# The value projection of the stick-breaking branch in 512 columns, two row tiles at a time

## The chip, the core and the metric

The kernel runs on one core of one Trainium2 chip. The metric is the device time of one execution in microseconds (us): the median of three runs, and beside it one execution that was taken with the hardware profiler, from which every row below comes. TensorE is called PE here, VectorE DVE, ScalarE ACT, GpSimd POOL, and SP is the engine that issues most transfers.

## What is computed

One layer of a decoder trunk on 512 tokens of width 1024. Cut to what matters for the change:

```python
h    = rms_norm(x, g_mix)                       # 512 x 1024
proj = h @ w_in                                 # 1024 x 5120
qa, ka, va, qb, kb, vb, gates = split(proj)     # each of the first six is 512 wide
ya = moba_attention(qa, ka, va)                 # 8 heads of 64
yb = stick_breaking_attention(qb, kb, vb)       # 8 heads of 64
m  = sigmoid(gate_a) * (ya @ W_a) + sigmoid(gate_b) * (yb @ W_b)
x  = x + m @ W_out                              # then a ConvGLU and a last RMSNorm
```

Here `vb`, the values of the second branch, is a product of 512 rows (four row tiles of 128) with 1024 x 512 weights. The change touches how this one product is cut up.

## The kernel before

Every large product is done three times, in pieces that keep float32 accuracy: each operand is split into a high and a low part, and `mm3` (lines 72 to 75) issues high x high, high x low, low x high into one PSUM tile. Weights come in blocks of 128 x 1024 float32 by one transfer each. `wload` (line 56) issues the transfer into a tile of the pool `wraw` (five deep), lets ACT write the high part (`whi`, line 68) and DVE the low part (`wlo`, line 69) into tiles of the pool `wsp` (three deep for each name, so a new block's split has to wait until PE is through with the block three loads earlier).

The middle of the kernel (63 to 240 us) weaves two kinds of work on PE. The attention proper is `attend`: for a pair of head pairs it goes through a list of nine pieces (scores of a group of query tiles, then turning the weights, at line 407) and ends with the product with the values (`av`, line 429). Between the pieces PE is given projections, as generators in the list `fillers`; `fill(n)` takes n steps from them. A step of 1.0 is three matmuls of 512 columns (the 256-column form of `vproj_b` yields 0.5 for three matmuls). The numbers n stand in GAPS_A, GAPS_A2 and GAPS_B. Order of the fillers: the second half of the first branch's q and k, q and k of pairs 0 and 1, `vproj_b(0)`, q and k of pairs 2 and 3, `vproj_b(1)`, and the first gate projections. PE's order is exactly the order in which the code is written (`manual_schedule`, line 50). The other engines' instructions are put in order by a scheduler that models their times when the program is built.

The projections write to PSUM tiles named `mm`, from `pmm`, two banks deep, used in turn. A third tile can be begun only when the first has been copied out. `vproj_b(g)` does half of the columns (256) for one row tile after the other: two row tiles share one bank, 48 matmuls, and are then copied out to `vb`, one half by ACT (line 251), one by DVE (line 252). So the bank of one pair of tiles is emptied while PE fills the other.

In the second branch DVE runs, for each group of scores, scans (line 378) and products (line 380) over the attention weights, after ACT's sigmoids (lines 364 and 366) and POOL's masks (line 370). DVE and ACT also empty the `av` tile into `ya` or `yb` (lines 435 and 436) and q and k of the second branch are copied out by DVE as `o` (lines 304 and 306).

Of the kernel before, what the change touches and what calls it, by code (L numbers as in the profile page):

```python
# [10 lines left out]
F32 = mybir.dt.float32  # L11
F32R = mybir.dt.float32r
BF = mybir.dt.bfloat16
AF = mybir.ActivationFunctionType
OP = mybir.AluOpType
# [3 lines left out]
S = 512  # L19
D = 1024  # L20
KT = D // 128
QT = S // 128
# [4 lines left out]
NWARM = 9 * (448,) + (128,)  # L27
NP = FT // 2
NL = 3
WORDER = ([(n, k) for n in ("qk0", "va") for k in range(4)] + [("vb", g, h) for g in range(2) for h in range(2)]  # L30
          + [("mqk", n, i) for n in range(2) for i in range(2)] + [("sqk", p, n) for p in range(4) for n in range(2)]
          + [("g", i, b) for i in range(KT) for b in range(2)] + [("ab", i) for i in range(KT)]
          + [("out", k) for k in range(KT)] + [("ox", j) for j in range(KT // 2)] + [("up", i, b) for i in range(FT) for b in range(2)]
# [6 lines left out]
def trunk_layer(ctx: ExitStack, tc: tile.TileContext, x: bass.AP, xT: bass.AP, w: bass.AP, vec: bass.AP,  # L40
                gfin: bass.AP, trig: bass.AP, out: bass.AP):
    nc = tc.nc

    def pool(stack, name, bufs, space=None, side=None):
        kw = {}
        if space is not None:
            kw["space"] = space
        if side is not None:
            kw["side"] = side
        return stack.enter_context(tc.tile_pool(name=name, bufs=bufs, reuse_waits="tile", **kw))  # L50
# [2 lines left out]
    consts = pool(ctx, "consts", 1)  # L53
    wraw = pool(ctx, "wraw", 5)
    wsp = pool(ctx, "wsp", 3)
    def wload(key, pieces=1, eng=None):
        raw = wraw.tile([128, 1024], F32, name="raw")
        hi = wsp.tile([128, 1024], F32R, name="whi")
        lo = wsp.tile([128, 1024], F32R, name="wlo")
        n = 1024 // pieces  # L60
        for i in range(pieces):
            sl = slice(i * n, (i + 1) * n)
            (eng if eng is not None and i == 0 else nc.sync).dma_start(raw[:, sl], w[WIDX[key]][:, sl])
            if eng is not None and i == 0:
                nc.scalar.preload_act_table_set("sqrt_and_others")
        for i in range(pieces):
            sl = slice(i * n, (i + 1) * n)
            nc.scalar.activation(hi[:, sl], raw[:, sl], AF.Copy)  # L68
            nc.vector.tensor_sub(lo[:, sl], raw[:, sl], hi[:, sl].bitcast(F32))  # L69
        return hi, lo  # L70

    def mm3(ps, a, b, start, stop, **kw):
        nc.tensor.matmul(ps, a[0], b[0], start=start, stop=False, **kw)  # L73
        nc.tensor.matmul(ps, a[0], b[1], start=False, stop=False, **kw)  # L74
        nc.tensor.matmul(ps, a[1], b[0], start=False, stop=stop, **kw)  # L75

    def blk(t, k, n=128):
        return t[0][:, k * n:(k + 1) * n], t[1][:, k * n:(k + 1) * n]
# [23 lines left out]
    xg = [hp.tile([128, 2, S], F32R, name=f"xg{k}") for k in range(KT)]  # L102
    rb = hp.tile([128, S], F32, name="rb")
    asta = ExitStack()
    vp = pool(asta, "vp", 1)
    vb = vp.tile([128, QT, 512], F32, name="vb")
# [27 lines left out]
    pmm = pool(psA, "pmm", 2, PSUM)  # L134
# [7 lines left out]
    qk0 = [p1.tile([128, S], F32, name=f"q{j}") for j in range(4)]  # L142
# [18 lines left out]
    for k in range(KT):  # L161
# [7 lines left out]
        else:  # L169
            if k % 2 == 0:  # L170
# [3 lines left out]
                                             op0=OP.mult, op1=OP.subtract)  # L174
# [60 lines left out]
        use(ps)  # L235
        yield 1.0

    def vproj_b(g):
        wt = tuple(wload(("vb", g, h)) for h in range(2))
        for t in range(QT):  # L240
            if t % 2 == 0:
                ps = pmm.tile([128, S], F32, name="mm")
            o = ps[:, (t % 2) * 256:(t % 2 + 1) * 256]
            for k in range(KT):
                a = (xg[k][:, 0, t * 128:(t + 1) * 128], xg[k][:, 1, t * 128:(t + 1) * 128])
                mm3(o, a, blk(wt[k // 4], k % 4, 256), k == 0, k == KT - 1)
                if k < KT - 1:
                    yield 0.5
            if t % 2:
                dst = vb[:, t - 1:t + 1, g * 256:(g + 1) * 256]  # L250
                nc.scalar.activation(dst[:, 0], ps[:, :256], AF.Copy, scale=r1[:, t - 1:t])
                nc.vector.tensor_scalar(dst[:, 1], o, r1[:, t:t + 1], None, op0=OP.mult)
            yield 0.5

    def fill(n):
        while n > 0 and fillers:
# [35 lines left out]
    def moba_qk(g):  # L292
        for n in range(2):
            half = {}
            for i in range(2):
                yield from proj(("mqk", n, i), lambda ps: rotate(g, n, i, ps, half))
# [146 lines left out]
    st1.close()  # L443
    atp = pool(asta, "atp", 2)
    att = pool(asta, "att", 2)
    psc = pool(psA, "psc", 2, PSUM)
    ptr = pool(psA, "ptr", 1, PSUM)
    def gates(i):
# [9 lines left out]
            yield from proj(("g", i, b), lambda ps: use(b, ps))  # L458

    pend = {}  # L460
    fillers = [moba_qk(1), sb_qk(0), sb_qk(1), vproj_b(0), sb_qk(2), sb_qk(3), vproj_b(1)]
    fillers += [gates(i) for i in range(NG)]
    GAPS_A = (12, 0, 5, 5, 0, 5, 7, 5, 5)
    GAPS_A2 = (10, 0, 3, 6, 0, 3, 6, 3, 3)
    GAPS_B = (8, 4, 5, 4, 3, 5, 7, 5, 5)
    attend("a", (0, 1), GAPS_A)
    attend("a", (2, 3), GAPS_A2, True)
# [2 lines left out]
    for p in range(4):  # L470
        yhl["b", p] = ybp.tile([128, 2, S], F32R, name=f"yb{p}")
    gsig = pool(ysta, "gsig", 6, side="right")
    attend("b", (0, 1), GAPS_B)
    attend("b", (2, 3), GAPS_B)
    fill(1000)
    psA.close()
# [3 lines left out]
    pmm = pool(psB, "pmm2", 6, PSUM)  # L480
# [390 lines left out]
def pack(w_in, w_a, w_b, w_out, w_up, w_down):  # L871
    def rows(m, c):
        return m[:, c].reshape(m.shape[0] // 128, 128, len(c)).transpose(1, 0, 2).reshape(128, -1)

    c128 = np.arange(128)
    t = {}

    def halves(base, g, i):
        return base + (4 * g + c128 // 32) * 64 + 32 * i + c128 % 32

    first = np.concatenate([halves(base, 0, i) for base in (0, 512) for i in range(2)])
    for k in range(4):
        t["qk0", k] = rows(w_in[k * 256:(k + 1) * 256], first)
    for n, base in enumerate((0, 512)):
        for i in range(2):
            t["mqk", n, i] = rows(w_in, halves(base, 1, i))
    for j in range(4):
        t["va", j] = rows(w_in[j * 256:(j + 1) * 256], 1024 + np.arange(512))
    for g in range(2):
        for h in range(2):  # L890
            t["vb", g, h] = rows(w_in[h * 512:(h + 1) * 512], 2560 + g * 256 + np.arange(256))
    for p in range(4):
        for n, base in enumerate((1536, 2048)):
            t["sqk", p, n] = rows(w_in, base + p * 128 + c128)
    for i in range(KT):
        for b in range(2):
            t["g", i, b] = rows(w_in, 3072 + b * 1024 + i * 128 + c128)
        t["ab", i] = np.concatenate([rows(w_a, i * 128 + c128), rows(w_b, i * 128 + c128)], axis=1)
        t["out", i] = w_out[i * 128:(i + 1) * 128]
    for j in range(KT // 2):  # L900
        t["ox", j] = np.concatenate([w_out[(2 * j + b) * 128:(2 * j + b + 1) * 128, 512:] for b in range(2)], axis=1)
    for i in range(FT):
        for b in range(2):
            t["up", i, b] = rows(w_up, b * FF + i * 128 + c128)
        t["down", i] = w_down[i * 128:(i + 1) * 128]
    for j in range(NP):
        t["dx", j] = np.concatenate([w_down[(2 * j + b) * 128:(2 * j + b + 1) * 128, 512:] for b in range(2)], axis=1)
    return np.ascontiguousarray(np.stack([t[k] for k in WORDER]))

# [27 lines left out]
```

## Time and profile before

| what | value |
|---|---|
| median of three runs | 724.46 us (724.16 to 724.82) |
| the profiled execution | 725.84 us |
| its span on the core | 724.1 us |
| PE busy in the span | 714.9 us, 99% |
| DVE busy in the span | 554.3 us, 77% |
| ACT busy in the span | 346.5 us, 48% |
| PE's share of the chain that ended last | 94% |

The profiled execution lies 1.4 us above the median, and 1.7 us of it lie outside the span. A matmul's listed time (some 390 ns at 512 columns) overlaps its neighbour's. What PE really takes for one is the distance from its start to the next one's start, so starts are compared in all that follows, and a PE that is busy at every moment is a PE that has no listed wait.

### The profile page before, as it was taken

What the parts mean: (1) busy time and instruction counts of PE and PEld (TensorE: products, weight loads), DVE (VectorE), ACT (ScalarE), POOL (GpSimd) and SP (SyncE); (2) the same over time, 40 slices, a digit from 0 to 9 for tenths busy, and PEclk for the clock granted to TensorE, in tenths of its full rate; (3) what the DMA queues carried; (4) which work ended last, traced back from release to release, by engine and by line L of the source; (5) the groups of instructions that cost most, each with busy time, mean ns of one, the idle gap of its engine ahead of it and who ended that gap; (6) DMA issues with size and microseconds to landing.
All of it is one profiled execution on the core that took longest, in us unless ns stands there. A gap on an engine that the chain in (4) does not pass through costs nothing.

```text
span 724.1 us, 9746 instructions
## 1 busy us (share of the span) xinstructions
PE 714.9 (99%) x3792; PEld 593.3 (82%) x3792; DVE 554.3 (77%) x796; ACT 346.5 (48%) x507; POOL 22.7 (3%) x40
## 2 busy tenths in 40 slices
PE   9999999999999999999999999999999999999996
PEld 6888888879888888888888888888888888788784
DVE  7678867594873654669878787787787789888997
ACT  6335435463663232337384444443444444556664
POOL 0000000230310000000000000000000000000000
PEclk9999999999999999999999999999999999999998
DMA  8522111021122323235744223223223323467703
GB/s 305 195 88 80 67 49 69 31 88 59 60 91 68 104 87 98 82 112 180 281 153 140 90 88 109 95 88 108 96 88 102 101 88 103 138 220 226 273 29 118
DMA packets 25679, 84.11 MB, mean 116 GB/s; under 512 B 2848, under 2 KB 3616, under 8 KB 25632
## 3 DMA queue, kind: packets, MB, share of 16 engines
q1 hardware_dynamic: 25344, 83.15, 34.0%
q8 instruction: 30, 0.49, 0.3%
q10 hardware_dynamic: 288, 0.33, 0.1%
q14 instruction: 17, 0.14, 0.1%
HBM read 79.27 MB, written 4.19 MB: 115 GB/s over the span
## 4 chain that ended last, share of the span: by engine, by line
PE 94%; DVE 3%; ACT 1%; DMA 1%; issue 0%; ACTq 0%
PE b L74 13%; PE b L75 12%; PE b L73 12%; PE mm L73 11%; PE mm L74 11%; PE mm L75 11%; PE c L74 4%; PE c L73 4%; PE c L75 4%; PE q L188 3%; PE tp L429 2%; PE tp L407 2%; PE sc L330 1%; PE sc L340 1%; DMA raw<-w 1%; PE v L74 1%
## 5 line engine op out<-in xcount | busy, mean ns | idle before, releaser
L68 ACT ACTIVATE whi<-raw 128x1024 fp32r<-128x1024 f32 (+2 forms) x98 | 98.2, 1008 | 167.5 <-PE b L74 80.7
L74 PE MATMUL b<-h,whi 128*128 128x512 f32 x352 | 137.1, 389 | 0.3 <-DVE h L634 0.3
L73 PE MATMUL b<-h,whi 128*128 128x512 f32 x352 | 137.1, 390 | 0.0
L75 PE MATMUL b<-h,wlo 128*128 128x512 f32 x352 | 136.9, 389 | 0.0
L69 DVE TENSOR_TENSOR wlo<-raw,whi 128x1024 fp32r<-128x1024 f32 (+2 forms) x98 | 112.9, 1157 | 14.6 <-ACT whi L68 14.4
L73 PE MATMUL mm<-xg,whi 128*128 128x512 f32 x224 | 89.9, 401 | 0.0
L75 PE MATMUL mm<-xg,wlo 128*128 128x512 f32 x224 | 87.4, 390 | 0.0
L74 PE MATMUL mm<-xg,whi 128*128 128x512 f32 x224 | 87.3, 390 | 0.0
L74 PEld LDWEIGHTS b<-h,whi 128*128 128x128 f32 x352 | 66.1, 188 | 14.2 <-DVE h L634 0.7
L75 PEld LDWEIGHTS b<-h,wlo 128*128 128x128 f32 x352 | 66.1, 188 | 13.8
L73 PEld LDWEIGHTS b<-h,whi 128*128 128x128 f32 x352 | 66.1, 188 | 13.6
L556 ACT ACTIVATE whi<-raw 128x1024 fp32r<-128x1024 f32 x45 | 46.6, 1051 | 34.0 <-DVE raw L568 21.1
L556 DVE TENSOR_TENSOR wlo<-raw,whi 128x1024 fp32r<-128x1024 f32 x45 | 54.3, 1218 | 4.4 <-ACT whi L556 4.4
L725 DVE TENSOR_TENSOR u<-b,rb 128x512 f32<-128x512 f32 x44 | 30.3, 691 | 30.4 <-PE b L75 30.3
L73 PEld LDWEIGHTS mm<-xg,whi 128*128 128x128 f32 x224 | 42.1, 188 | 10.2 <-issue 1.8
L75 PEld LDWEIGHTS mm<-xg,wlo 128*128 128x128 f32 x224 | 42.0, 188 | 9.1
L74 PEld LDWEIGHTS mm<-xg,whi 128*128 128x128 f32 x224 | 42.2, 188 | 7.8
L727 ACT ACTIVATE t<-u,vecs 128x512 f32<-128x512 f32 x44 | 35.2, 802 | 2.1 <-DVE u L725 2.1
L74 PE MATMUL c<-wlo,xa 128*128 128x512 f32 x88 | 34.3, 390 | 0.4 <-DVE wlo L556 0.4
L73 PE MATMUL c<-whi,xa 128*128 128x512 f32 x88 | 34.2, 389 | 0.0
L75 PE MATMUL c<-whi,xa 128*128 128x512 f32 x88 | 34.2, 389 | 0.0
L730 DVE SCALAR_TENSOR_TENSOR t<-u,vecs,t 128x510 f32<-128x510 f32 x44 | 32.9, 749 | 1.3
(222 smaller groups left out, 1261.6 us busy)
## 6 DMA issues: line engine op xcount, KB each, us to landing
raw<-w SPq DMA_DIRECT2D x133, 512.0 KB, 3.3
xk<-xT SPq DMA_DIRECT2D x8, 256.5 KB, 5.3
x<-x SPq DMA_DIRECT2D x4, 512.0 KB, 7.1
x1D<-x SPq DMA_DIRECT2D x8, 256.0 KB, 3.4
x1R<-x1D SPq DMA_DIRECT2D x4, 512.0 KB, 8.0
raw<-w SPq DMA_DIRECT2D x6, 256.0 KB, 5.8
out<-on SPq DMA_DIRECT2D x6, 256.0 KB, 2.3
tg<-trig SPq DMA_DIRECT2D x1, 512.0 KB, 6.8
```

What stands on the lines that cost most here:

```text
L68: nc.scalar.activation(hi[:, sl], raw[:, sl], AF.Copy)
L69: nc.vector.tensor_sub(lo[:, sl], raw[:, sl], hi[:, sl].bitcast(F32))
L73: nc.tensor.matmul(ps, a[0], b[0], start=start, stop=False, **kw)
L74: nc.tensor.matmul(ps, a[0], b[1], start=False, stop=False, **kw)
L75: nc.tensor.matmul(ps, a[1], b[0], start=False, stop=stop, **kw)
L188: nc.tensor.matmul(qk0[c], w0[i][:, (k % 2) * 512 + c * 128:(k % 2) * 512 + (c + 1) * 128], xg[k][:, j], start=(k == 0 and n == 0), stop=( ...
L407: nc.tensor.transpose(tp[:, h, c:c + 128], a[:, h, c:c + 128], ident)
L429: nc.tensor.matmul(av[h * 64:(h + 1) * 64, j, qt * 128:(qt + 1) * 128], v[:, kb, (2 * p + h) * 64:(2 * p + h + 1) * 64], aT[p][:, h, o + k ...
L556: splits.append((nc.scalar.activation(hi, raw, AF.Copy), nc.vector.tensor_sub(lo, raw, hi.bitcast(F32))))
L725: nc.vector.tensor_mul(u, ps, rb2)
L727: nc.scalar.activation(t, u, AF.Identity, bias=cb[:, c:c + 1], scale=cw[:, 2, c:c + 1])
L730: nc.vector.scalar_tensor_tensor(t[:, 2:], u[:, :S - 2], cw[:, 0, c:c + 1], t[:, 2:], op0=OP.mult, op1=OP.add)
```

## The change

`vproj_b` takes no half any more. It does all 512 columns, for two row tiles (`T` = 0: tiles 0 and 1, then `T` = 1: tiles 2 and 3) that each fill one of the two banks of `pmm` at the same time. It goes through the four weight blocks (256 rows of the weights each, 512 columns), and with each block does the first tile, then the second. The blocks are loaded in the first round and kept for the second: three in `wsp`, the fourth in a pool of its own, `vbw`. There are 96 matmuls of 512 columns where there were 192 of 256. A round ends with a copy of the first tile by ACT and of the second by DVE, each 128 x 512, and the next round begins in the same two banks. The weights are packed in another shape to match; the number and size of the transfers stay. All of `vproj_b` stands ahead of q and k of pairs 2 and 3 in `fillers`, and the first pass of the second branch has its own, larger gaps (52 steps in place of 46), so that those projections are done by its end.

```diff
-WORDER = ([(n, k) for n in ("qk0", "va") for k in range(4)] + [("vb", g, h) for g in range(2) for h in range(2)]
+WORDER = ([(n, k) for n in ("qk0", "va", "vb") for k in range(4)]
...
-    def wload(key, pieces=1, eng=None):
+    def wload(key, pieces=1, eng=None, p=wsp):
         raw = wraw.tile([128, 1024], F32, name="raw")
-        hi = wsp.tile([128, 1024], F32R, name="whi")
-        lo = wsp.tile([128, 1024], F32R, name="wlo")
+        hi = p.tile([128, 1024], F32R, name="whi")
+        lo = p.tile([128, 1024], F32R, name="wlo")
...
-    def vproj_b(g):
-        wt = tuple(wload(("vb", g, h)) for h in range(2))
-        for t in range(QT):
-            if t % 2 == 0:
-                ps = pmm.tile([128, S], F32, name="mm")
-            o = ps[:, (t % 2) * 256:(t % 2 + 1) * 256]
-            for k in range(KT):
-                a = (xg[k][:, 0, t * 128:(t + 1) * 128], xg[k][:, 1, t * 128:(t + 1) * 128])
-                mm3(o, a, blk(wt[k // 4], k % 4, 256), k == 0, k == KT - 1)
-                if k < KT - 1:
-                    yield 0.5
-            if t % 2:
-                dst = vb[:, t - 1:t + 1, g * 256:(g + 1) * 256]
-                nc.scalar.activation(dst[:, 0], ps[:, :256], AF.Copy, scale=r1[:, t - 1:t])
-                nc.vector.tensor_scalar(dst[:, 1], o, r1[:, t:t + 1], None, op0=OP.mult)
-            yield 0.5
+    def vproj_b():
+        wts = []
+        for T in range(2):
+            ps = [pmm.tile([128, S], F32, name="mm") for _ in range(2)]
+            for j in range(4):
+                if T == 0:
+                    wts.append(wload(("vb", j), p=vbw if j == 3 else wsp))
+                for i in range(2):
+                    t = 2 * T + i
+                    for k in range(2 * j, 2 * j + 2):
+                        a = (xg[k][:, 0, t * 128:(t + 1) * 128], xg[k][:, 1, t * 128:(t + 1) * 128])
+                        mm3(ps[i], a, blk(wts[j], k % 2, 512), k == 0, k == KT - 1)
+                        if k < KT - 1:
+                            yield 1.0
+                    if j == 3:
+                        if i:
+                            nc.vector.tensor_scalar(vb[:, t], ps[i], r1[:, t:t + 1], None, op0=OP.mult)
+                        else:
+                            nc.scalar.activation(vb[:, t], ps[i], AF.Copy, scale=r1[:, t:t + 1])
+                        yield 1.0
...
+    vbw = pool(asta, "vbw", 1)
+    vbw.tile([128, 12], F32, name="gap")
...
-    fillers = [moba_qk(1), sb_qk(0), sb_qk(1), vproj_b(0), sb_qk(2), sb_qk(3), vproj_b(1)]
+    fillers = [moba_qk(1), sb_qk(0), sb_qk(1), vproj_b(), sb_qk(2), sb_qk(3)]
...
+    GAPS_B1 = (8, 4, 6, 5, 3, 6, 8, 6, 6)
     GAPS_B = (8, 4, 5, 4, 3, 5, 7, 5, 5)
...
-    attend("b", (0, 1), GAPS_B)
+    attend("b", (0, 1), GAPS_B1)
```

Three pieces of the instruction order, before and after; numbers behind a name tell tiles apart.

Place 1, PE, where the projection of pair 1's k ends and `vproj_b` begins, in the first branch's last pass. Before (`mm_1229` is that k, `mm_1333` the first pair of row tiles, `tp_1346` a turning of weights), around the first turning behind it:

```order
L75 MATMUL mm_1333<-whi_1322,xg3_95 128x256
L407 MATMUL tp_1346<-ident_67,a1_1197 128x128 x6
L73 MATMUL mm_1333<-whi_1328,xg4_96 128x256
L74 MATMUL mm_1333<-wlo_1329,xg4_96 128x256
L75 MATMUL mm_1333<-whi_1328,xg4_96 128x256
L73 MATMUL mm_1333<-whi_1328,xg5_97 128x256
```

After (`mm_1233` is that k, `mm_1325` and `mm_1326` are row tiles 0 and 1, which share the block `whi_1328`):

```order
L75 MATMUL mm_1233<-xg7_99,wlo_1229 128x512
L73 MATMUL mm_1325<-whi_1328,xg0_92 128x512
L74 MATMUL mm_1325<-wlo_1329,xg0_92 128x512
L75 MATMUL mm_1325<-whi_1328,xg0_92 128x512
L73 MATMUL mm_1325<-whi_1328,xg1_93 128x512
L74 MATMUL mm_1325<-wlo_1329,xg1_93 128x512
L75 MATMUL mm_1325<-whi_1328,xg1_93 128x512
L411 MATMUL tp_1339<-ident_67,a1_1201 128x128 x6
L73 MATMUL mm_1326<-whi_1328,xg0_92 128x512
L74 MATMUL mm_1326<-wlo_1329,xg0_92 128x512
L75 MATMUL mm_1326<-whi_1328,xg0_92 128x512
```

Before, the work behind the turning goes on in the tile begun ahead of it. After, it begins a second tile, `mm_1326`, which takes the bank that `mm_1233` had.

Place 2, PE, at the start of the second branch's first pass, behind its first scores. Before (`mm_1404` is the second pair of row tiles, `mm_1598` the next projection, q of pair 2):

```order
L73 MATMUL mm_1404<-whi_1328,xg7_99 128x256
L74 MATMUL mm_1404<-wlo_1329,xg7_99 128x256
L75 MATMUL mm_1404<-whi_1328,xg7_99 128x256
L73 MATMUL mm_1598<-xg0_92,whi_1593 128x512
L74 MATMUL mm_1598<-xg0_92,whi_1593 128x512
L75 MATMUL mm_1598<-xg0_92,wlo_1594 128x512
```

After (`mm_1326` is row tile 1, `mm_1558` and `mm_1559` are row tiles 2 and 3):

```order
L73 MATMUL mm_1326<-whi_1412,xg7_99 128x512
L74 MATMUL mm_1326<-wlo_1413,xg7_99 128x512
L75 MATMUL mm_1326<-whi_1412,xg7_99 128x512
L73 MATMUL mm_1558<-whi_1328,xg0_92 128x512
L74 MATMUL mm_1558<-wlo_1329,xg0_92 128x512
L75 MATMUL mm_1558<-whi_1328,xg0_92 128x512
L73 MATMUL mm_1558<-whi_1328,xg1_93 128x512
L74 MATMUL mm_1558<-wlo_1329,xg1_93 128x512
L75 MATMUL mm_1558<-whi_1328,xg1_93 128x512
L73 MATMUL mm_1559<-whi_1328,xg0_92 128x512
```

Before, a new tile begins in the bank that had been left 48 matmuls earlier. After, `mm_1559` begins six matmuls behind the end of `mm_1326`, whose bank it takes.

Place 3, DVE, in the same stretch. Before (`R` are the scans, `a2` the products with them, `ya2` and `ya3` the results of the first branch):

```order
L436 TENSOR_TENSOR ya2_87<-tp_1451,ya2_87 128x512
L378 SCALAR_TENSOR_TENSOR R_1548<-a1_1536 128x128
L436 TENSOR_TENSOR ya3_88<-tp_1451,ya3_88 128x512
L378 SCALAR_TENSOR_TENSOR R_1548<-a1_1536 128x128
L378 SCALAR_TENSOR_TENSOR R_1548<-a1_1536 128x256 x2
L380 TENSOR_TENSOR a2_1538<-a2_1538,R_1548 128x2x128
L380 TENSOR_TENSOR a2_1538<-a2_1538,R_1548 128x2x256
L378 SCALAR_TENSOR_TENSOR R_1569<-a1_1557 128x128 x2
L378 SCALAR_TENSOR_TENSOR R_1569<-a1_1557 128x256 x2
L252 TENSOR_SCALAR vb_104<-mm_1404,n1r_339 128x256
```

After:

```order
L440 TENSOR_TENSOR ya2_87<-tp_1424,ya2_87 128x512
L382 SCALAR_TENSOR_TENSOR R_1521<-a1_1509 128x128
L440 TENSOR_TENSOR ya3_88<-tp_1424,ya3_88 128x512
L382 SCALAR_TENSOR_TENSOR R_1521<-a1_1509 128x128
L382 SCALAR_TENSOR_TENSOR R_1521<-a1_1509 128x256 x2
L384 TENSOR_TENSOR a2_1511<-a2_1511,R_1521 128x2x128
L254 TENSOR_SCALAR vb_104<-mm_1326,n1r_339 128x512
L384 TENSOR_TENSOR a2_1511<-a2_1511,R_1521 128x2x256
```

The copy of a `vb` tile stands behind the first product with the scans after the change, and stood four scans and one product later before it. Both copies stand behind all the scans of the first pair.

## Rows read from the trace of the kernel before

**Rows 1.** Window: length, PE busy (instructions), granted clock, transfer share, GB/s.

```profile
60.00:240.00 180.00, 180.00 (x1381) 1.00 0.20 65
```

**Rows 2.** PE by time, a stretch of 256 columns: start, length, instruction, count.

```profile
119.51 0.82 PE L407 MATMUL tp<-ident,a 128*128 128x128 f32 x6
120.08 0.36 PE L73 MATMUL mm<-whi,xg 128*128 128x256 f32 x1
...
124.47 1.03 PE L407 MATMUL tp<-ident,a 128*128 128x128 f32 x8
125.26 0.36 PE L73 MATMUL mm<-whi,xg 128*128 128x256 f32 x1
```

**Rows 3.** PE by time, a stretch of 512 columns.

```profile
110.51 0.48 PE L73 MATMUL mm<-xg,whi 128*128 128x512 f32 x1
...
114.73 0.82 PE L407 MATMUL tp<-ident,a 128*128 128x128 f32 x6
```

**Rows 4.** PE by time, undisturbed stretches of either width.

```profile
104.09 0.39 PE L73 MATMUL mm<-xg,whi 128*128 128x512 f32 x1
...
104.77 0.39 PE L73 MATMUL mm<-xg,whi 128*128 128x512 f32 x1
...
121.47 0.28 PE L75 MATMUL mm<-whi,xg 128*128 128x256 f32 x1
...
121.83 0.28 PE L75 MATMUL mm<-whi,xg 128*128 128x256 f32 x1
```

**Rows 5.** DVE by time, behind the last scores of the first branch.

```profile
117.40 2.36 DVE L348 TENSOR_REDUCE st<-sc 128x2 f32<-128x1024 f32 x2 [2.80 <-PE sc L330]
119.67 0.68 DVE L306 TENSOR_TENSOR o<-mm,rb 128x512 f32<-128x512 f32 x1
...
121.26 1.22 DVE L69 TENSOR_TENSOR wlo<-raw,whi 128x1024 fp32r<-128x1024 f32 x1
```

**Rows 6.** PE by time, where vproj_b begins, and around av and the first scores.

```profile
118.09 0.28 PE L73 MATMUL mm<-whi,xg 128*128 128x256 f32 x1
...
130.60 4.59 PE L429 MATMUL tp<-aT,va 128*64 128x128 f32 x80
...
136.69 0.39 PE L73 MATMUL mm<-whi,xg 128*128 128x256 f32 x1
```

**Rows 7.** DVE by time, the first scores of the second branch.

```profile
138.46 0.60 DVE L378 TENSOR_TENSOR_SCAN R<-a 128x128 f32<-128x128 f32 x1 [1.91 <-POOL a L370]
138.99 0.66 DVE L436 TENSOR_TENSOR ya<-tp,ya 128x512 fp32r<-128x512 f32 x1
139.57 1.90 DVE L378 TENSOR_TENSOR_SCAN R<-a 128x128 f32<-128x128 f32 x3
141.39 1.36 DVE L380 TENSOR_TENSOR a<-a,R 128x256 f32<-128x256 f32 x2
```

**Rows 8.** Groups of DVE instructions, 30 to 245 us: shapes, count, busy us, mean ns, idle.

```profile
L380 DVE TENSOR_TENSOR a<-a,R 128x256 f32<-128x256 f32 x4 | 2.1, 536 | 0.0
L215 DVE TENSOR_SCALAR va<-mm,n1r 128x512 f32<-128x512 f32 x1 | 0.8, 751 | 0.6 <-PE mm L75 0.6
```

**Rows 9.** A wait of PE on DVE elsewhere, DVE and PE by time.

```profile
32.17 0.69 DVE L131 COPY rb<-mm 128x512 f32<-128x512 f32 x1 [1.66 <-PE mm L130]
...
32.92 0.50 PE L73 MATMUL mm<-whi,xg 128*128 128x512 f32 x1
```

**Rows 10.** Windows at the end (columns PE, PEld, DVE, ACT, POOL, clock), and PE at the start.

```profile
716.00:720.00 4.00, 1.31 (x6) 0.75 (x4) 3.28 (x12) 2.46 (x6) 0.00 (x0) 1.00 0.76 292
720.00:724.10 4.10, 0.00 (x0) 0.00 (x0) 0.29 (x1) 0.35 (x1) 0.00 (x0) 0.56 0.34 133
...
1.30 3.65 PE L145 MATMUL mm<-warmb 128*128 128x448 bf16 x10 [1.30 <-DVE R L375]
5.12 2.99 PE L188 MATMUL q<-xg,whi 128*128 128x512 f32 x8 [0.17 <-ACT whi L68]
...
8.86 1.98 PE L188 MATMUL q<-xg,whi 128*128 128x512 f32 x8
```

More of the change, by code (lines that the diff above doesn't have):

```diff
@@ L887, in pack @@
     for j in range(4):
[L888 to L891, printed above, removed]
+        for n, base in (("va", 1024), ("vb", 2560)):
+            t[n, j] = rows(w_in[j * 256:(j + 1) * 256], base + np.arange(512))
     for p in range(4):
```

## The prediction

> **What bounds the kernel now.** I read the page's shares first, then PE's waits, then PE and DVE by time around the places that the change touches. PE is busy for all of the 180 us from 60 to 240 us, at the full granted clock [rows 1]: in the whole stretch in which `vproj_b` runs, nothing that DVE, ACT, POOL or a transfer does holds PE up. So time is won there only by making PE's own work shorter, and every wait of PE that the change brings is lost in full, because behind it there is no idle time that could shrink.
>
> **What the change takes off PE.** 192 matmuls of 256 columns become 96 of 512. The columns streamed are the same, so the gain can only be what a matmul costs beside its columns. Undisturbed, three of 256 go from 121.47 to 121.83, 0.120 us each, and three of 512 from 104.09 to 104.77, 0.227 us each [rows 4]. Then 192 x 0.120 = 23.0 us become 96 x 0.227 = 21.8 us, 1.3 us less. With the turnings in between, 36 of 256 take from 120.08 to 124.47, 4.39 us [rows 2], and 18 of 512, the same work, from 110.51 to 114.73, 4.22 us [rows 3]; this is 0.17 us per 36, times 192/36 is 0.9 us. The first ignores the slower starts behind a turning and the second takes one stretch with much traffic for all. I take 1.0 us and keep 0.9 to 1.3.
>
> The Trainium skill, "TensorE: Matmul & The Clock Gate", section "Back-to-back issue gap", has a rule that speaks against even this gain: the columns divided by 2.4 GHz plus a fixed 2.5 ns for each matmul. By that, an estimate, 96 matmuls fewer would save only 0.24 us, and the sum below would come out 0.8 us higher, at 727.8. The rows show about 13 ns over the columns' own time at both widths (0.120 against 0.107, 0.227 against 0.213), so the measurement decides.
>
> **What costs nothing.** The transfers keep size, number and order. The third block's split takes the `wsp` slot that PE leaves with pair 1's k, where q of pair 2 was split before. That split ended on DVE at 121.26 + 1.22 = 122.48 [rows 5]; PE will want it two blocks after the start, at about 125.4, so work of 2.9 us hides it. The fourth block, in `vbw`, waits for no slot and is split long ahead. q of pair 2 can be split when the second round has left the first block, 12 steps before PE needs it. ACT's copy at the end of each round has at least two steps and a turning (or all of `av`) before its bank is wanted. Four copies of 512 columns replace eight of 256. The three projections that come later than before still end before `av` of the first pass of the second branch, whose 4.5 us [rows 6] cover the last splits of pair 3. The gates only move up; PE has no wait there for them to remove.
>
> **Place 1, a new wait: tile 1's bank.** Two tiles at once need both banks at once. Row tile 1 (`mm_1326`) takes the bank of pair 1's k, which has ended only two steps and one turning before. DVE empties it (line 306) behind two reductions: from 119.67 for 0.68, to 120.35 [rows 5]. The reductions wait on scores that the change doesn't move. PE gets there sooner: `vproj_b` begins at 118.09 [rows 6], six matmuls at 0.227 bring it to 119.45, and a turning of six takes 0.57 as from 119.51 to 120.08 [rows 2], so PE is ready at 120.02. Elsewhere a matmul starts 0.06 us after the DVE copy that frees its bank has ended (32.17 + 0.69 = 32.86, and 32.92) [rows 9]. So PE goes on at 120.41: **0.4 us lost**, bounds 0.2 (PE comes later by slower matmuls) to 0.6 (a longer handover).
>
> **Place 2, the large one: tile 3's bank.** At the start of the second branch PE does the last two steps of row tile 1, two steps of tile 2, and then wants tile 1's bank for tile 3 (`mm_1559`). DVE has 6 matmuls' time, 1.36 us, to copy 128 x 512 out. The one such copy measured takes 0.75 us [rows 8], so it would fit if DVE did it at once. But DVE works in its built order, and there the copy stands behind the result of the first branch, four scans and a product of the first head pair. The first scan begins at 138.46, when POOL's mask is done, the four scans end about 141.5, and the two overlapping products start at 141.39 [rows 7]. This chain hangs on `av` (ACT's copy, then sigmoid, mask and scan), and `av` moves little: by place 1 PE has lost 0.4 and won some 0.3 until then, so it begins 0.1 later than 130.60 [rows 6].
>
> When does PE want the bank? Filler work behind the scores began at 136.69 [rows 6], now 136.80. Six matmuls at 0.227 with 0.1 us more for the first behind another shape (as 18 of 512 took 4.22 behind a turning where 18 x 0.227 is 4.09 [rows 3]) take 1.46, six more 1.36: 139.62. When does it get it? The first product, at 536 ns a piece [rows 8], takes from 141.39 to about 141.85 with the overlap of its successor; the copy then 0.75, and the handover 0.06: 142.66, with the shift 142.77. **3.1 us lost**, bounds 2.7 (a copy of 0.5, the product short) and 3.4 (PE's tiles turn up 0.3 sooner). Behind the waiting matmul stand the next scores and, through them, the sigmoids; they move by the same 3.1 us and wait for nobody new. On ACT the split of q of pair 2 now waits for PE's fourth step of the second round, ahead of those sigmoids, and is through before the scores arrive.
>
> Before the change this copy stood even further back on DVE, but nobody waited: a bank had 48 matmuls of 256, some 5.8 us, and another projection behind it.
>
> **The sum.** -1.0 + 0.4 + 3.1 = +2.5 us. Against the profiled execution's own 725.84 that is 728.3; its 1.4 us above the median are the profile's, so the forecast for the median is 724.46 + 2.5 = **727.0**. Its own range is -1.3 + 0.2 + 2.7 = +1.6 to -0.9 + 0.6 + 3.4 = +3.1, which is 726.1 to 727.6.
>
> **Rivals.**
> - The copy comes in time. If DVE's chain of scans started 3 us sooner against PE, or PE came 3 us later, place 2 would cost nothing and only place 1 remain: 724.46 - 1.0 + 0.4 = 723.9; with that gone too, 723.5, faster by 0.1%. It decides at a copy ending before 139.6. Against it: the first scan alone starts at 138.46 [rows 7] and four follow. For it: the order of DVE is read from the program, the times from a trace of another order. To be called faster the gain must reach 0.2%, 1.45 us, about what a measurement of this kernel can tell from no change; 1.3 is what the columns give at most, so this case ends faster by that bound only with a gain that I don't see, and mostly as no change. 0.10.
> - The waits are partly paid back, because what piled up on DVE and ACT while PE stood makes later pieces run more freely. Then PE would have to have waits to lose, and it has none [rows 1]. A half of 3.1 paid back gives 725.5. 0.07.
> - The clock falls. PE stands for about 3 us at full clock, which it does nowhere between 60 and 240 us. That it can fall is seen at the end of the kernel: after PE's last six matmuls, at the front of the window from 716 to 720, the granted clock is 1.00 in that window and 0.56 in the next, on its way to the lower level (1.2 GHz against 2.4) [rows 10]. At the start PE began at 1.30; eight matmuls took 2.99 us from 5.12 and 1.98 from 8.86 [rows 10], so the low level held up to some 6 us from there, in which half of the time is lost: 3 us more, 730.0. Against it: no stretch of this trace shows a fall while PE still has work. 0.10.
>   The Trainium skill, "TensorE: Matmul & The Clock Gate", section "Part 1: The HAM clock gate", says that an idle TensorE is taken down to half its clock and must be busy again before it gets it back; the end of this trace agrees, and no row here shows it in the middle of a kernel.
>
> **How the numbers follow.** The forecast has 0.73, the three rivals 0.27. Slower by over 0.2%: nearly all of the forecast, for its lower end lies 0.2 us beyond that bound, and all of the clock case, 0.81. Faster by over 0.2%: the part of the first rival in which the columns give more than I see, 0.04. Within 0.2%: the rest of it, the case of waits paid back and an edge of the forecast, 0.15. The range runs from 725.4, which takes in the case paid back, to 728.6, for a wait half as long again or a short spell of the lower clock; a full one and the copy in time, together 0.2, are left out.
>
> **What the profile after would show.** One PE wait on DVE at the copy of `vb`, near 139.6, listed as some 3 us (a little less, since the last matmul still drains), and one of a few tenths on line 306's successor near 120.0; no others between 60 and 240. 96 matmuls of 128x512 with `xg` moving out of `whi` at 0.227 us start to start. The granted clock at 1.00 throughout. Wrong would be: no wait at the copy (the first rival), a matmul distance of 0.43 us behind it (the clock), or a wait of PE on ACT or on `wlo` in the projections behind.

## The result, and the profile after

| kernel | median, us | lowest to highest | ratio to the kernel before, 95% interval |
|---|---|---|---|
| before, beside it | 724.64 | 724.16 to 724.98 | |
| changed | 729.63 | 729.54 to 729.87 | 1.0068 [1.0056, 1.008] |
| changed, a second time (before, beside it: 724.91) | 729.13 | 728.70 to 730.14 | 1.006 [1.0046, 1.0074] |

The change costs 4.2 to 5.0 us, not 2.5: slower, as forecast, but outside the range, which ended at 728.6. The profiled execution took 729.71 us, with a span of 728.0.

The first view answers [rows 1]: the same window, after. Columns: length, PE busy (matmuls), PEld, DVE, ACT, POOL, granted clock, transfer share, GB/s.

```profile
60.00:240.00 180.00, 176.89 (x1265) 145.30 (x1265) 123.47 (x189) 85.74 (x139) 19.96 (x32) 0.99 0.20 65
```

PE is short of 3.1 us of work, and the clock reads 0.99 where it read 1.00. PE's list of waits for that window has one line (total, times, longest):

```profile
PE mm L73 <- DVE vb L254: 2.9, 1, 2.9
```

That is place 2, the forecast wait for tile 1's copy. PE by time around it, and DVE by time, which answers [rows 7]:

```profile
138.44 0.39 PE L74 MATMUL mm<-wlo,xg 128*128 128x512 f32 x1
138.67 0.39 PE L75 MATMUL mm<-whi,xg 128*128 128x512 f32 x1
141.97 0.50 PE L73 MATMUL mm<-whi,xg 128*128 128x512 f32 x1 [2.91 <-DVE vb L254]
142.30 0.40 PE L74 MATMUL mm<-wlo,xg 128*128 128x512 f32 x1
142.53 0.59 PE L75 MATMUL mm<-whi,xg 128*128 128x512 f32 x1
142.93 0.63 PE L73 MATMUL mm<-whi,xg 128*128 128x512 f32 x1
143.35 0.63 PE L74 MATMUL mm<-wlo,xg 128*128 128x512 f32 x1
...
145.49 0.62 PE L73 MATMUL mm<-whi,xg 128*128 128x512 f32 x1
145.91 0.42 PE L74 MATMUL mm<-wlo,xg 128*128 128x512 f32 x1
146.18 0.40 PE L75 MATMUL mm<-whi,xg 128*128 128x512 f32 x1
146.50 0.62 PE L344 MATMUL sc<-hl,hl 64*128 64x384 f32 x4
```

```profile
137.78 0.60 DVE L382 TENSOR_TENSOR_SCAN R<-a 128x128 f32<-128x128 f32 x1 [1.91 <-POOL a L374]
138.30 0.66 DVE L440 TENSOR_TENSOR ya<-tp,ya 128x512 fp32r<-128x512 f32 x1
138.88 1.90 DVE L382 TENSOR_TENSOR_SCAN R<-a 128x128 f32<-128x128 f32 x3
140.70 0.55 DVE L384 TENSOR_TENSOR a<-a,R 128x256 f32<-128x256 f32 x1
141.18 0.74 DVE L254 TENSOR_SCALAR vb<-mm,n1r 128x512 f32<-128x512 f32 x1
```

From 138.67 to 141.97 is 3.30 us where a matmul takes 0.23: 3.07 us lost. The copy stands on DVE where the forecast put it, and PE goes on 0.05 us after its end (141.18 + 0.74 = 141.92). The times fit too. This trace runs 0.67 us ahead of the one before already at `vproj_b`'s first matmul (117.42, against 118.09 in [rows 6]), ahead of all that the change does on PE; with 0.67 added, PE wants the bank at 139.57 and gets on at 142.64, where the forecast had 139.62 and 142.77.

Now read on past the wait. The first two matmuls behind it come as ever, but from 142.53 to 145.91 the distance is 0.40 to 0.43 us instead of 0.23. The windows show it as clock (columns as in the first view):

```profile
139.00:142.00 3.00, 0.09 (x2) 0.03 (x1) 3.00 (x6) 0.86 (x2) 2.88 (x5) 1.00 0.00 0
142.00:146.00 4.00, 4.00 (x11) 3.14 (x12) 3.75 (x10) 1.06 (x1) 0.00 (x0) 0.57 0.00 0
146.00:150.00 4.00, 4.00 (x25) 3.00 (x24) 2.02 (x3) 2.07 (x3) 1.31 (x2) 1.00 0.44 130
```

A PE that is listed as busy for all of 4.00 us did 11 matmuls there, at a granted clock of 0.57 over the window. The six distances from 143.35 to 145.91 are 0.427 us on average, nearly twice the 0.227 of [rows 4], and the granted clock from 143 to 145 is 0.50: the lower of TensorE's two levels, 1.2 GHz instead of 2.4. The 12 matmuls of tile 3 take 146.50 - 141.97 = 4.53 us. In a profile without the fall (the first experiment) the same 12 take 2.95, so the clock costs 1.58 us. No list of waits shows this, since PE waited for nobody.

Three smaller losses don't appear among the waits either, since matmuls' listed times overlap; they show in the starts. Place 1, which answers [rows 2]; DVE's copy that frees the bank, which answers [rows 5]:

```profile
118.80 0.82 PE L411 MATMUL tp<-ident,a 128*128 128x128 f32 x6
119.73 0.50 PE L73 MATMUL mm<-whi,xg 128*128 128x512 f32 x1
```

```profile
119.00 0.68 DVE L310 TENSOR_TENSOR o<-mm,rb 128x512 f32<-128x512 f32 x1
```

The copy ends at 119.68, PE goes on at 119.73, 0.93 us after the turning began and not 0.57: 0.36 us lost. So the loss of place 1 came as forecast, but not its sign, a listed wait. The second is a turning of pairs 2 and 3, PE and ACT by time:

```profile
215.46 0.39 PE L75 MATMUL mm<-xg,wlo 128*128 128x512 f32 x1
215.92 0.88 PE L411 MATMUL tp<-ident,a 128*128 128x128 f32 x6
```

```profile
213.53 0.72 ACT L460 ACTIVATE g<-g,vecs 128x512 f32<-128x512 f32 x1 [1.77 <-DVE g L459]
214.16 1.01 ACT L370 ACTIVATE a<-sc 128x1024 f32<-128x1024 f32 x1
215.07 0.80 ACT L414 ACTIVATE aT<-tp 128x768 f32<-128x768 f32 x1
```

The distance is 0.46 us where 0.23 is usual (at the same step before, 207.96 to 208.19). The turning waits for ACT's copy of the one before it, which ends at 215.87 behind two sigmoids. One of them (line 460) belongs to a gate, which the change moved up into this stretch; that this sigmoid is what makes the copy late is argued from the order on ACT, no run took it out by itself. Last, the first product with `yb`:

```profile
237.28 0.39 PE L75 MATMUL mm<-ya,wlo 128*128 128x512 f32 x1
237.59 0.47 PE L73 MATMUL mm<-yb,whi 128*128 128x512 f32 x1
237.90 0.40 PE L74 MATMUL mm<-yb,whi 128*128 128x512 f32 x1
```

Two distances of 0.31 in place of 0.23 are 0.17 us; before, the first three `yb` matmuls stood 0.23 apart (233.79, 234.02, 234.24).

The ledger from the trace: width -0.87 (the distances in `vproj_b` add up to 23.73 us for 192 matmuls before and to 27.51 for 96 after, less 3.07 and 1.58), place 1 +0.36, place 2 +3.07, clock +1.58, turning +0.24, first product +0.17: **+4.55 us**, against +4.99 and +4.2 measured. The two profiled spans differ by 3.9 us (728.0 and 724.1), which is this sum less the 0.67 us that the trace after was ahead at the start.

### The profile page after: what moved, and what is told of

The parts are those of the page before. It is cut to its first block, busy times and chain, and to the rows that moved or that the text cites. A ratio compares the mean times of both kernels' runs of the same rounds, so it can differ in the third digit from the quotient of the medians.

```text
span 728.0 us, 9546 instructions
## 1 busy us (share of the span) xinstructions
PE 715.8 (98%) x3696; PEld 588.8 (81%) x3696; DVE 553.5 (76%) x794; ACT 346.5 (48%) x505; POOL 21.0 (3%) x40
## 4 chain that ended last, share of the span: by engine, by line
PE 60%; issue 26%; DVE 8%; ACT 3%; DMA 3%; POOL 1%; DVEq 0%; POOLq 0%; ACTq 0%
PE b L74 12%; PE b L75 12%; PE b L73 12%; PE mm L73 6%; PE mm L75 6%; PE mm L74 6%; DMA raw<-w 3%; DVE wlo L563 2%; PE c L73 1%; PE c L75 1%; PE c L74 1%; DVE raw L575 1%; DVE R L382 1%; ACT whi L563 1%; POOL a L374 1%
## 5 line engine op out<-in xcount | busy, mean ns | idle before, releaser
L382 DVE TENSOR_TENSOR_SCAN R<-a 128x128 f32<-128x128 f32 (+3 forms) x32 | 26.2, 870 | 10.7 <-POOL a L374 10.7
```

Of the source, the lines that this page charges most:

```text
L382: nc.vector.tensor_tensor_scan(R[:, h, r0:r0 + n][:, ::-1], z[:, ::-1], z, 1.0, op0=OP.mult, op1=OP.bypass)
```

## The experiments

**Theory A**: the loss is the stop of PE at place 2 and, as a cost of its own behind it, the clock. **Rivals**: the clock falls at any stop, or for another reason than idleness (B); stop and clock don't carry the loss (C); the moved order of the fillers costs (D). The kernel before took 724.84, 724.91 and 724.75 us beside the three groups of runs.

**Another engine copies tile 1.**

```diff
-                        if i:
+                        if t == 3:
                             nc.vector.tensor_scalar(vb[:, t], ps[i], r1[:, t:t + 1], None, op0=OP.mult)
                         else:
                             nc.scalar.activation(vb[:, t], ps[i], AF.Copy, scale=r1[:, t:t + 1])
```

> The changed kernel with one edit: row tile 1's finished v is copied out of its bank by ACT and not by DVE. TensorE's order stays the same. In the changed kernel TensorE stands 2.91 us before tile 3's first matmul, until DVE's copy of tile 1, and then its matmuls start every 0.427 us for 3.4 us, at a granted clock of 0.5. On ACT the copy stands behind four sigmoids that end at 139.86 us; with 0.69 us for the copy it ends at 140.5 to 140.6, so TensorE resumes near 140.7 and not at 141.97: idle 1.5 to 1.7 us. Theory A (the stop is the copy's place in DVE's queue, and the clock falls because the stop is long): gain 1.3 us from the shorter stop and 1.6 us from the clock that holds, so 729.63 - 2.9 = 726.7 us. Theory B (the clock falls after any stop of TensorE here): only the 1.3 us, 728.3 us. Theory C (neither the stop nor the clock carries the loss): no change, 729.4 to 729.8 us.

Measured: 726.33 us (725.66 to 726.79), ratio 1.0022 [1.0012, 1.0031]. PE's order is the same, the stop is half as long, and the clock holds:

```profile
138.32 0.39 PE L75 MATMUL mm<-whi,xg 128*128 128x512 f32 x1
140.14 0.50 PE L73 MATMUL mm<-whi,xg 128*128 128x512 f32 x1 [1.43 <-ACT vb L256]
140.47 0.39 PE L74 MATMUL mm<-wlo,xg 128*128 128x512 f32 x1
...
142.77 0.39 PE L75 MATMUL mm<-whi,xg 128*128 128x512 f32 x1
143.09 0.61 PE L344 MATMUL sc<-hl,hl 64*128 64x384 f32 x4
```

From 140.14 to 143.09 are the 2.95 us used above. Two costs of different kinds went with one edit: 1.5 us of the stop, and the clock. C falls, and of B the first half, since PE stops here too and the clock holds.

**A stop of 2.2 us.** The second round takes its tiles in this order:

```diff
+            for i, k in ([(0, 0), (0, 1), (0, 2), (1, 0), (1, 1), (1, 2)] + [(i, k) for k in range(3, KT) for i in range(2)] if T else
...
```

> The changed kernel with another order of the second pair of row tiles: tile 2 goes through its first three blocks of 128 rows of xg before tile 3 begins, so three matmuls (3 x 0.227 = 0.68 us) stand between the first pair's end and the wait for tile 1's copy that stood behind it before. The copy's place on DVE stays. The idle time goes from 2.91 to about 2.2 us, the copy's end from its spot stays. Theory A, if a stop of 2.2 us still takes the clock: 729.63 - 0 us; the work moved ahead only fills the stop, so the gain is 0.68 us: 728.95 us, granted clock 0.5 for some 3.4 us. If a stop of 2.2 us does not take the clock: 728.95 - 1.6 = 727.35 us. Theory C (the loss isn't here): 729.4 to 729.8 us.

Measured: 728.09 us, ratio 1.0041 [1.0028, 1.0055], but the five executions fall apart: 726.35 and 726.67 us at a mean granted clock of 0.997 and 0.998, and 728.09, 728.65 and 729.00 at 0.994 to 0.995. PE's waits in the profiled one, which is the one of 726.67:

```profile
PE mm L73 <- DVE vb L251: 2.2, 1, 2.2
```

```profile
142.00:146.00 4.00, 4.00 (x24) 3.01 (x25) 3.93 (x10) 2.01 (x3) 0.07 (x1) 1.00 0.02 4
```

Where the clock held, 24 matmuls stand in the window that had 11. Both outcomes that had been expected as alternatives came, in the same program, each somewhat lower than worked out (726.5 for 727.35, 728.6 for 728.95). A fallen execution was not profiled here; that the other group is the clock's is read from its mean clock, and its 2.1 us (means of 728.6 and 726.5) are more than the 1.58 of the trace above. Why, stays open.

**No stop, by an earlier first pair.**

```diff
-    GAPS_A2 = (10, 0, 3, 6, 0, 3, 6, 3, 3)
-    GAPS_B1 = (8, 4, 6, 5, 3, 6, 8, 6, 6)
+    GAPS_A2 = (10, 0, 3, 6, 0, 3, 6, 3, 5)
+    GAPS_B1 = (6, 4, 6, 5, 3, 6, 8, 6, 6)
```

> The changed kernel with two units of filler moved from behind the first scores of the second branch to the end of the branch before: the first pair of row tiles then ends before the step of the weighted sums (av), and DVE's copy of tile 1 comes while DVE has little to do, ahead of the scans. Theory A (the stop of 2.91 us and the clock's fall behind it, 1.6 us, are the change's whole loss beside some 0.8 us of small waits): no stop near 139 us, granted clock 1.00 from 60 to 240 us, 729.63 - 3.07 - 1.58 = 725.0 us (724.7 to 725.3), that is within 0.1% of the kernel before. Theory C (another place of the new order is what costs): 727 us or more. Whether width then shows as a gain over the kernel before (0.87 us saved against 0.36 us at the first bank and 0.2 to 0.5 us of small waits) is told by the sign of what is left: -0.3 to +0.5 us.

Measured: 724.61 us (723.79 to 724.88), ratio 0.9996 [0.9987, 1.0005]; no wait in PE's list from 60 to 240 us, clock 1.00. DVE by time:

```profile
131.65 0.75 DVE L254 TENSOR_SCALAR vb<-mm,n1r 128x512 f32<-128x512 f32 x1 [2.19 <-PE mm L75]
```

The same copy comes at 131.65, on a DVE that had stood idle for 2.19 us, and the kernel is level with the one before. Two numbers of a table are worth what the change lost. Level does not mean that nothing is lost any more: place 1 (119.07 to 120.00), the turning and the first `yb` product still start late, 0.77 us together, and the distances in `vproj_b` add up to 22.71 us where they were 23.73, 1.02 less.

**No stop, by one tile after the other.** The second round does tile 2 through all eight blocks of `xg`, then tile 3.

```diff
+            for i, k in ([(i, k) for i in range(2) for k in range(KT)] if T else
...
```

> The changed kernel with its second pair of row tiles done one tile after the other: all eight blocks of 128 rows for tile 2, then all eight for tile 3. DVE's copy of tile 1 stays where it stands, behind the scans, and ends near 141.9 us, but it is asked for 20 matmuls (4.5 us) of tile 2, 18 of them new in this place, and a set of scores later. Theory A: no stop, clock 1.00, 729.6 - 3.07 - 1.6 = 724.9 us, or 724.6 us by what the removal of the stop gave before. A theory that DVE's order itself (the copy behind the scans and the products that wait for it) costs TensorE time elsewhere: over 726 us.

Measured: 724.22 us (723.83 to 725.53), ratio 0.9993 [0.9984, 1.0001], no wait in PE's list, clock 1.00. DVE's copy of tile 1, and tile 3's first matmul:

```profile
141.54 0.74 DVE L251 TENSOR_SCALAR vb<-mm,n1r 128x512 f32<-128x512 f32 x1
144.82 0.39 PE L73 MATMUL mm<-whi,xg 128*128 128x512 f32 x1
```

The copy stays behind the scans on DVE and ends at 142.28, and nobody misses it, since PE wants the bank only 2.5 us later: the late place costs only because PE asked early.

**The moved order alone, 256 columns wide.**

```diff
-    fillers = [moba_qk(1), sb_qk(0), sb_qk(1), vproj_b(0), sb_qk(2), sb_qk(3), vproj_b(1)]
+    fillers = [moba_qk(1), sb_qk(0), sb_qk(1), vproj_b(0), vproj_b(1), sb_qk(2), sb_qk(3)]
...
-    attend("b", (0, 1), GAPS_B)
+    attend("b", (0, 1), (8, 4, 6, 5, 3, 6, 8, 6, 6))
```

> The kernel before with its two stretches of v of the second branch left 256 columns wide and with one piece of the change: both stand one after the other, ahead of the products of pairs 2 and 3, and the branch's first call has the changed kernel's table of gaps. It has no wider v, no second pair of banks held at once, and the copies are of 256 columns. Theory A (the loss comes from holding two banks over the scans, not from the moved order): 724.64 us + 0 to 0.6 us of small waits = 724.6 to 725.3 us, clock 1.00 from 60 to 240 us. Theory D (the moved order is what costs, whatever the width): a stop of 2 us or more at the first scores of the second branch, 727 to 730 us. The changed kernel's time less this one's is what width and the pairs of banks cost.

Measured: 724.95 us (724.46 to 725.79), ratio 1.0003 [0.9994, 1.0011]. D falls: with a bank for each pair of narrow tiles the new order brings no stop, and by the interval it costs 0.8 us at most. The late turning (210.98 to 211.46) and the slow start of the first `yb` product (232.81, 233.13, 233.43) are in this trace too, 0.41 us together by the distances of the ledger, so both belong to the order and not to the width.

**The changed kernel again, and the stop filled with idle work.**

> The changed kernel once more, unedited, on the chip of the runs it is compared with. If the stop of 2.91 us always takes the clock: all its executions near 729.5 us (729.0 to 730.0), granted clock 0.5 for some 3.4 us behind the stop near 139 us. If it only takes it in some executions, as the stop of 2.2 us did (726.35 and 726.67 us in two, 728.09 to 729.00 us in three): two groups, near 727.5 and near 729.5 us.

Measured: 729.13 us, 728.70 to 730.14. One group: none of the nine executions of this kernel so far lies under 728.70. Two of them were profiled, and both show the fall; for the other seven it is read from their times. The second profile has it in another place:

```profile
141.78 0.80 PE L73 MATMUL mm<-whi,xg 128*128 128x512 f32 x1 [2.94 <-DVE vb L254]
142.38 0.63 PE L74 MATMUL mm<-wlo,xg 128*128 128x512 f32 x1
...
145.30 0.39 PE L75 MATMUL mm<-whi,xg 128*128 128x512 f32 x1
```

```profile
141.60:141.80 0.20, 0.02 (x1) 0.02 (x1) 0.20 (x2) 0.00 (x0) 0.09 (x1) 1.00 0.00 0
141.80:142.00 0.20, 0.20 (x1) 0.20 (x2) 0.20 (x1) 0.00 (x0) 0.00 (x0) 0.50 0.00 0
```

Here the low level begins with the first matmul behind the stop, some 0.6 us sooner than in the first profile. The price is the same: tile 3's 12 matmuls take 4.52 us (141.78 to 146.30), 1.57 us more than the 2.95.

The stop filled: the kernel does 12 matmuls in it whose result nobody reads.

```diff
             ps = [pmm.tile([128, S], F32, name="mm") for _ in range(2)]
+            for n in range(12 * T):
+                nc.tensor.matmul(ps[0], xg[0][:, 0, :128], blk(wts[0], 0, 512)[0], start=True, stop=True)
```

> The changed kernel with 12 matmuls of 128 x 128 by 128 x 512 more, whose result nobody reads: they write the bank of row tile 2 before its first true product and stand in TensorE's order just there, in the place of the stop. 12 x 0.22 us are 2.6 to 2.7 us, so TensorE waits 0.2 to 0.3 us and not 2.91 us for DVE's copy of tile 1, and its useful work resumes when it did, near 142 us. Theory A (two separate costs: the stop itself, 3.07 us, and the clock behind it, 1.6 us or more): the stop's loss stays, the clock holds at 1.00, and the gain is the clock's share alone: 729.6 - 1.6 = 728.0 us by the trace, 727.2 us if the clock's fall costs the 2.2 us by which the slower executions of the kernel with the 2.2 us stop lay above its faster ones. If the fall of the clock has another cause than TensorE's idleness: 729.5 us, clock 0.5 there as before. If the stop's length was not what cost: under 726 us.

Measured: 727.38 us (727.22 to 727.86), ratio 1.0034 [1.0022, 1.0047]; 1.75 us less than the changed kernel beside it, and no execution of the one overlaps the other's. PE by time, then the window:

```profile
137.13 2.89 PE L243 MATMUL mm<-whi,xg 128*128 128x512 f32 x12
...
140.99 0.39 PE L75 MATMUL mm<-whi,xg 128*128 128x512 f32 x1
141.59 0.50 PE L73 MATMUL mm<-whi,xg 128*128 128x512 f32 x1 [0.22 <-DVE vb L256]
141.93 0.39 PE L74 MATMUL mm<-wlo,xg 128*128 128x512 f32 x1
```

```profile
142.00:146.00 4.00, 4.00 (x25) 3.02 (x24) 3.93 (x10) 1.55 (x2) 0.00 (x0) 1.00 0.01 4
```

The 12 matmuls stand six matmuls ahead of the wait and take 2.72 us (137.13 to 139.85); the wait itself is left with 0.37 us over a usual distance. So useful work is held up for 3.09 us as before, but the clock holds and 25 matmuls stand where 11 did. That is the clock by itself: 1.75 us. What is left of the loss against the kernel without a stop is 727.38 - 724.61 = 2.8 us, the stop itself (from two groups of runs, with a scatter of some tenths). The second half of B falls: the clock's fall hangs on PE being idle, since matmuls without use prevent it in all five executions (mean clock 0.998).

**The small waits removed as well.** The earlier first pair, and two edits more:

```diff
+            for i, k in ([(i, k) for j in range(4) for i in range(2) for k in (2 * j, 2 * j + 1)] if T else
+                         [(0, 0), (0, 1), (0, 2), (1, 0), (1, 1), (1, 2)] + [(i, k) for k in range(3, KT) for i in range(2)]):
...
-    GAPS_B = (8, 4, 5, 4, 3, 5, 7, 5, 5)
+    GAPS_B = (8, 4, 5, 4, 3, 6, 6, 5, 5)
```

> The changed kernel with three edits that move nothing but TensorE's order: the two units of filler moved ahead of the weighted sums, which took 5.0 us off; tile 0 goes through three blocks of 128 rows before tile 1 begins, so that the bank that pair 1's k leaves is asked for 0.68 us later (a loss of 0.36 us there); and in the second branch's second call one unit of filler moved from the sixth to the fifth pause but one, so that the transposes come 0.68 us later there (a loss of 0.24 us, behind ACT's copy of the transposes before). If both small waits are where the width's gain went: 724.61 - 0.36 - 0.24 = 724.0 us, 0.1% under the kernel before. If they only come back elsewhere: 724.6 us. If the weights of the second block come late, now that they are asked for 0.68 us sooner: 725 to 726 us.

Measured: 723.94 us (723.24 to 724.70), ratio 0.9986 [0.9977, 0.9994]. It is faster than the changed kernel and, by an interval that ends at 0.9994, than the kernel before. Place 1 and the turning, PE by time:

```profile
119.00 0.82 PE L411 MATMUL tp<-ident,a 128*128 128x128 f32 x6
119.58 0.48 PE L73 MATMUL mm<-whi,xg 128*128 128x512 f32 x1
...
211.19 0.39 PE L75 MATMUL mm<-xg,wlo 128*128 128x512 f32 x1
211.42 0.82 PE L411 MATMUL tp<-ident,a 128*128 128x128 f32 x6
```

0.58 us in place of 0.93, 0.23 in place of 0.46: both waits are gone and did not come back: 0.6 us by the starts, 0.7 us by the ratios (0.9996 to 0.9986), whose intervals overlap. The slow start of the first `yb` product is still there.

**The width by itself.** The last version again, beside the kernel before with the same order of fillers and the same gaps, 256 columns wide.

```diff
-    fillers = [moba_qk(1), sb_qk(0), sb_qk(1), vproj_b(0), sb_qk(2), sb_qk(3), vproj_b(1)]
+    fillers = [moba_qk(1), sb_qk(0), sb_qk(1), vproj_b(0), vproj_b(1), sb_qk(2), sb_qk(3)]
...
-    GAPS_A2 = (10, 0, 3, 6, 0, 3, 6, 3, 3)
-    GAPS_B = (8, 4, 5, 4, 3, 5, 7, 5, 5)
+    GAPS_A2 = (10, 0, 3, 6, 0, 3, 6, 3, 5)
+    GAPS_B = (8, 4, 5, 4, 3, 6, 6, 5, 5)
...
-    attend("b", (0, 1), GAPS_B)
+    attend("b", (0, 1), (6, 4, 6, 5, 3, 6, 8, 6, 6))
```

> The fastest version again, beside a version of the same order in 256 columns. If its gain is more than scatter: 0.1% under the kernel before once more, 723.9 us where the kernel before takes 724.9.

> The kernel before, 256 columns wide, with the order of the fillers and all the tables of gaps that the fastest version has: what is left between the two is the width (96 matmuls of 512 columns for 192 of 256) and nothing else of note. If the width gives what the traces show (0.87 us in v's own matmuls, forecast 1.0): this one 0.8 to 1.1 us slower than the fastest version, that is 724.7 to 725.0 us and level with the kernel before. If the gain came from the moved fillers and pauses alone: the same time as the fastest version, 723.9 us.

Measured: wide 723.68 us (723.23 to 724.53), ratio 0.9986 [0.9977, 0.9995]; narrow 724.51 (724.18 to 725.29), ratio 0.9998 [0.9989, 1.0007]. The width is worth 0.83 us by the medians, and 0.97 us by the starts (the distances in `vproj_b` add up to 23.68 us in the narrow trace and 22.71 in the wide one); the order without it is worth nothing that can be told from scatter.

## Why the prediction was wrong

| step of the prediction | forecast, us | from the trace | by experiments |
|---|---|---|---|
| width | -1.0 (0.9 to 1.3) | -0.87; -0.97 in the pair of traces without a stop | -0.83 |
| place 1 | +0.4 (0.2 to 0.6) | +0.36 | with the turning, 0.7 |
| place 2, the stop | +3.1 (2.7 to 3.4) | +3.07 | +2.8 |
| the clock behind it | 0 in the sum; a rival of +3.0 at 0.10 | +1.58 | +1.75 |
| turning behind a gate's sigmoid, first `yb` product | "The gates only move up", 0 | +0.41 | turning: with place 1, above; product: not removed |
| sum | +2.5 | +4.55 | +4.99 and +4.2 measured |

**What held.** PE bounds this stretch, and nothing of the stop is seen to be paid back: useful work loses 3.07 us in the trace, and the 2.8 us of the runs agree within their scatter. The three terms of the sum were right in place, and place 1 and place 2 in size, place 2 with the instruction, the engine that it waits for and the queue in front of it; that is the mechanism, not luck. Width was forecast at 1.0 with bounds from 0.9; it came out at 0.97 in the one pair of traces, and at 0.87 and 0.83, just under the bounds, in the other two readings. The rule of the Trainium skill that was weighed there ("TensorE: Matmul & The Clock Gate", "Back-to-back issue gap"; by it, an estimate, 0.24 us for 96 matmuls fewer) is too small here: 0.83 us are measured, nearly 9 ns for each matmul saved. That section gives the formula for a single matmul by itself and says that in a stream the weight loads count too.

**The step that failed** is the sentence "Against it: no stretch of this trace shows a fall while PE still has work", and with it "The granted clock at 1.00 throughout". The trace of before has no stop of PE of this length between 60 and 240 us, so it could not show a fall; its silence was read as evidence against. The one place where it does show PE going idle, the end of the kernel [rows 10], shows the clock falling. The mechanism was named, but as a rival at 0.10, and the range took in only "a short spell" of it. The fall alone, at the 1.58 us of the trace, would have put the forecast of 727.0 at 728.6, the very end of the range; with the smaller miss below it lies outside. What would have been right is a term in the sum: a stop of about 3 us, which the forecast itself held for the likeliest case, with the fall behind it.

Its price was off the other way: 3.0 from the start of the kernel [rows 10], where the low level held for some 6 us; here it held from 142.53 to 145.91, 3.4 us, and cost about half of that. The Trainium skill, "TensorE: Matmul & The Clock Gate", says in "Part 1: The HAM clock gate" that an idle TensorE goes to half its clock and must work to get it back; both traces agree for the middle of a kernel too. It also gives 426.7 ns for 512 columns at the lower level (under "Wait — 56ns, not 53.3ns?"), which is the 0.427 us of the rows from 143.35 to 145.91.

**The smaller miss**, 0.4 us: moved fillers were looked at for what they take away and not for what they put on ACT. A gate needs a sigmoid, on the same queue as the turnings' copies. And, by the order of the instructions, work that once stood behind the second branch's `av` no longer covers the copy of its result.

## What to carry to other kernels

When a tile gets a second accumulator, ask which engine empties the bank and what stands in front of that copy in its queue; the cure here was the order of PE's work and not the width: the first pair two steps earlier, or tile 3 begun 18 matmuls and a set of scores later. Three matmuls later did not do, and another engine for the copy took away only half of the stop. A stop of PE of some three us cost half as much again as its length here, by the times in all nine executions, and one of 2.2 us seems to have cost more than its length in some, because the clock fell; the fall belongs in the sum as a term, and where the stop can't be avoided, matmuls without use put into it can keep the clock. A fall of the clock is in no list of waits: look at starts of like matmuls behind every long wait, and at the granted clock there.

## What had not been expected of the hardware

The clock did not fall in the middle of the stop but at its end or behind it, and not at a fixed distance: in one profile the first two matmuls after 141.97 ran at full pace, and then eight distances were 0.40 to 0.43 us, while PE had work without a break; in the other the first matmul behind the stop was slow already. Nor does the program alone seem to decide whether it falls: with a stop of 1.43 us none of ten executions shows a fall (mean clock 0.997 to 0.999, within 1.2 us of each other), with 2.23 us three of five seem to, with 2.91 us two profiles do and seven more by their times. What sets it at 2.2 us, the runs don't tell.
